# A per-token factor sent to all partitions through DRAM in place of TensorE transposes, in a streaming encoder layer

## The chip, the cores and the metric

The kernel runs on one NeuronCore of one Trainium2 chip. The metric is the device time of one launch, in microseconds (us); the median of 3 runs before the change is 784.9 us (784.69 to 785.13). Engines: PE is TensorE (PEld its weight loads), DVE VectorE, ACT ScalarE, POOL GpSimd, and SP SyncE, which issues all DMAs of this kernel from one queue, in order.

## The reference

One post-norm layer over 2048 prompt frames and 128 sample frames (8 streams of 16), width 1024. One input projection feeds three branches; their gated results are concatenated and go through one output projection. Branch C is the one that the change touches:

```python
h = jnp.einsum('btd,de->bte', x, w_in)
a, g_a, u, v, g_b, c1, c2, g_c = jnp.split(h, SPLITS, axis=-1)
...
c = c1 * jax.nn.sigmoid(c2)
conv_ext = jnp.concatenate([conv_left.astype(c.dtype), c], axis=1)
y_c = conformer_tail(conv_ext, conv_w, conv_b, conv_ln_g, conv_ln_b, conv_pw_w, conv_pw_b)
...
def conformer_tail(ext, conv_w, conv_b, ln_g, ln_b, pw_w, pw_b):
    y = lax.conv_general_dilated(ext, conv_w[:, None, :].astype(ext.dtype), (1,), 'VALID',
                                 dimension_numbers=('NWC', 'WIO', 'NWC'),
                                 feature_group_count=D_CONV) + conv_b
    y = jax.nn.silu(layer_norm(y, ln_g, ln_b))
    return jnp.einsum('btc,ce->bte', y, pw_w) + pw_b
```

The convolution has 31 taps for each of the 384 channels. The layer norm over the channels needs, for each token, the factor 1/sigma = (var + eps)^-0.5 of them.

## The kernel before

**Tiles and blocks.** The 17 tiles of 128 tokens are cut into three blocks (6, 6 and 5 tiles; 768, 768 and 640 tokens). In a block the projection runs over 8 groups of weight columns: groups 0 and 1 make `c1` and `c2` (`ps_c`), 2 and 3 branch A (`ps_ga`, `ps_a`), 4 to 6 branch B, 7 the gate of C. Every product is made of three (high x high, low x high, high x low: L208, L209, L210), since the operands are split into two parts. PE writes the 512-column PSUM banks of the pool `psm`, of which there are six. A last stage runs the output projection tile by tile (`ps_o`, 16 weight slices x 3 products of 512 columns a tile), adds, normalises (L413 to L424, gain and bias on DVE) and stores `o_y`.

**Branch C.** Channels lie on the partitions. DVE does the 31 taps (`acc` from `cext`, and from `cexts` for the sample tokens, so that block 2 has two rows of taps that take turns). What follows the convolution of a block, its tail, is put between the products of the next block, and block 2's tail between those of the output stage. `tail_steps` yields its steps, and `spread` emits one of them every 3.9 us of modelled PE time (4.4 us in the output stage). A tail works on two halves of its block (384 tokens each; 256 in the last half of block 2):

- `sums`, `centre`: sum over the three channel tiles, a product with ones for the mean (`ps_mean`), centred values `dc`, their squares on ACT (`csq`) and the sum of these on DVE (`csqs`).
- `variance` (L572 to L595): for each 128 tokens a product of `csqs` as weights with one column of ones gives the sum over channels in a column of `ps_var`, token by token on the partitions (L577). ACT scales and adds eps (`cvar`, L588), POOL raises to the power -0.5 (L589), and ACT writes each token's number across a row of 128 (`crs`, L594).
- `scale` (L597 to L605): PE transposes `crs`, 128 tokens at a time (`ps_rstd`, L600), so that the numbers lie along the free dimension on all partitions, and DVE multiplies `dc` by them.
- `gate`, `pointwise`: SiLU on ACT, split into `shi` and `slo`, products `ps_pw`, store into `mix`.

The steps were in the order: variance of half 0, an empty step, scale of half 0, variance of half 1, an empty step, scale of half 1. `one` puts its one-column products 0.2 us of modelled time apart, so that long products come between them.

**What sets the order.** Each engine runs its instructions in the order in which the program emits them. `after(us, fn)` emits work when the modelled PE time has come that far. Nothing moves while the kernel runs: an instruction that waits holds up all behind it on its engine, and a DMA that waits holds up all behind it on SP. Weights of later blocks come back from DRAM (`whi<-keep`, `wlo<-keep`, L195) into a ring of 6 buffers, the first half of each odd group into `stage`.

The lines that the steps below name: L131 is the helper that records every DVE operation, L152 the ACT half of a split, L195 the loads of kept weights, L952 the loads of `mix`, L1021 POOL's addition of the bias to `xr`.

Of the kernel before, what the change touches and what calls it, by code (L numbers as in the profile page):

```python
# [9 lines left out]
F32 = mybir.dt.float32  # L10
F32R = mybir.dt.float32r
AF = mybir.ActivationFunctionType
ALU = mybir.AluOpType

D = 1024
P = 128
# [44 lines left out]
def splits(total):  # L61

    tiles = total // P
    n = -(-tiles // 3)
    out, t = [], 0
    for i in range(n):
        w = -(-(tiles - t) // (n - i))
        out.append((t * P, w * P))
        t += w
    return out  # L70
# [3 lines left out]
def encoder_kernel(ctx: ExitStack, tc: tile.TileContext, a):  # L74
    nc = tc.nc
# [5 lines left out]
    pst = ctx.enter_context(tc.tile_pool(name="pst", bufs=2, space=PS))  # L81
    dram = ctx.enter_context(tc.tile_pool(name="dram", bufs=1, space=bass.MemoryType.DRAM))
# [13 lines left out]
    def after(us, fn):  # L96
        Clock.seq += 1
        heapq.heappush(events, (Clock.pe + us, Clock.seq, fn))
# [35 lines left out]
    vec = Vector()  # L134
# [155 lines left out]
    for k in range(2):  # L290
        nc.vector.tensor_copy(whi0[:, k, :], w0[:, k, :])
        nc.vector.tensor_tensor(out=wlo0[:, k, :], in0=w0[:, k, :], in1=whi0[:, k, :].bitcast(F32),
                                op=ALU.subtract)
# [17 lines left out]
    ident = const.tile([P, P], F32, name="ident")  # L311
# [4 lines left out]
    onef = ones.bitcast(F32)  # L316
# [3 lines left out]
    cp = ctx.enter_context(tc.tile_pool(name="convp", bufs=1))  # L320
# [214 lines left out]
    def tail_steps(b):  # L535

        st = {}
# [34 lines left out]
        def variance(i, t0, n):  # L572

            ps = pst.tile([P, 384], F32, tag="tr", name="ps_var")
            nt = n // P
            def one(t):
                nc.tensor.matmul(ps[:, t:t + 1], st["sq", i][:, t * P:(t + 1) * P], onef[:, 0:1],  # L577
                                 start=True, stop=True)
                if t + 1 < nt:
                    after(0.2, lambda: one(t + 1))  # L580
                else:
                    after(0.4, go)
            v = const.tile([P, 3], F32, tag="cvar", bufs=2, name="cvar")[:, :nt]
            rb = cp.tile([P, 384], F32, tag="s", bufs=2, name="crs").rearrange("p (i t) -> p i t", t=P)
            st["rs", i] = rb

            def go():
                nc.scalar.activation(out=v, in_=ps[:, :nt], func=AF.Identity, scale=1.0 / 384, bias=eps)  # L588
                nc.gpsimd.tensor_tensor(out=v, in0=v, in1=mhalf.to_broadcast([P, nt]), op=ALU.pow)  # L589
                after(1.2, wide)  # L590

            def wide():
                for t in range(nt):
                    nc.scalar.activation(out=rb[:, t, :], in_=onef, func=AF.Identity, scale=v[:, t:t + 1])  # L594
            one(0)  # L595

        def scale(i, t0, n):  # L597
            ps = pst.tile([P, 384], F32, tag="tr", name="ps_rstd")
            for t in range(n // P):
                nc.tensor.transpose(ps[:, t * P:(t + 1) * P], st["rs", i][:, t, :], ident)  # L600

            def go():
                for j in range(3):
                    vec.tensor_tensor(out=d[:, j, t0:t0 + n], in0=d[:, j, t0:t0 + n], in1=ps[:, :n], op=ALU.mult)
            after(0.4, go)  # L605

        def gate(t0, n, j):
            s = cp.tile([P, 384], F32, tag="s", bufs=2, name="s")
# [24 lines left out]
        todo = splits(len(BLOCKS[b]) * P)  # L633
        d = cp.tile([P, 3, TMAX], F32, tag="dc", name="dc")
# [5 lines left out]
            fn()  # L640
        for i, (t0, n) in enumerate(todo):
            yield lambda: variance(i, t0, n)
            yield None
            yield lambda: scale(i, t0, n)
        for t0, n in todo:
            for j in range(3):
# [242 lines left out]
    for b in range(len(BLOCKS)):  # L889
        if b > 0:  # L890
            drain()
            conv_state["held"] = []
            spread(tail_steps(b - 1))
# [24 lines left out]
        elif b < LASTB:  # L918
# [4 lines left out]
            def load(*ks, b=b):  # L923
                for k in ks:
                    rows[k] = XRow(b + 1, k)
# [16 lines left out]
    op = ctx.enter_context(tc.tile_pool(name="outp", bufs=1, reuse_waits="tile"))  # L942
# [128 lines left out]
    for q in range(2):  # L1071
        out_finish(q, both[q], True)
    tail = tail_steps(LASTB)
    nxt = Mixed(3)
    for q in range(2, NTILE):
# [86 lines left out]
```

## Time and profile before

| | |
|---|---|
| median of 3 runs | 784.9 us |
| the profiled execution | 785.07 us |
| its span | 783.4 us |
| mean granted TensorE clock | 0.998 |
| DVE's taps (L131, `acc`) | 270 in the largest group, 258.2 us |
| one-column products (`ps_var`) | 34 passes, median 208 ns |
| transposes (`ps_rstd`) | 17, median 272 ns |
| ACT's rows of 128 (`crs`) | 17, median 388 ns |

The span is what the trace covers; the rest of the time lies around it. The views used below: the busy shares by engine; the chain of work that ended last; the waits by engine; the timeline, in which a row gives the start, the time, the engine, the line, the operation, the result and its sources, how many were merged, and in brackets the idle time before and what ended it; the rows of one tile (minimum/median/maximum ns, first and last start); the DMA issues (how many, KB each, median us from issue to landing). Busy times of PE overlap, since its products are pipelined: what one product costs is read from the distance of the starts.

### The profile page before, as it was taken

How to read it: one execution, taken by the hardware profiler on the slowest of the kernel's cores; microseconds unless marked ns; L12 is line 12 of the kernel's file. 1: busy time of each engine (PE TensorE's matmuls, PEld its weight loads, DVE VectorE, ACT ScalarE, POOL GpSimd, SP SyncE). 2: the span in 40 equal slices, each digit the busy share in tenths (PEclk: the TensorE clock that was granted, in tenths of full speed). 3: DMA queues.
4: the chain of work that ended last, by engine and by line, in shares of the span. 5: the costliest groups of instructions: out<-in, count | busy, mean ns of one | idle time of the engine just before them, and what ended most of it. 6: DMA issues, size and time to landing. Idle time of an engine off the chain costs nothing.

```text
span 783.4 us, 11336 instructions
## 1 busy us (share of the span) xinstructions
PE 771.0 (98%) x4340; PEld 732.5 (94%) x4340; DVE 611.6 (78%) x899; ACT 203.2 (26%) x379; POOL 144.2 (18%) x172
## 2 busy tenths in 40 slices
PE   8999999999999999999999999999999999999996
PEld 6999999999999999999999999999988878888885
DVE  5799999996489989896047888899764997676665
ACT  5322324222312130220142122031351243131210
POOL 1010112210001011230002200151006254232341
PEclk9999999999999999999999999999999999999999
DMA  7966856459531465413656147362377334435311
GB/s 248 342 216 190 284 208 236 159 188 338 183 109 44 90 231 193 161 45 138 228 169 208 47 94 219 144 209 97 134 239 267 108 134 162 161 110 182 128 69 73
DMA packets 74774, 132.91 MB, mean 170 GB/s; under 512 B 15584, under 2 KB 41312, under 8 KB 74720
## 3 DMA queue, kind: packets, MB, share of 16 engines
q1 hardware_dynamic: 74720, 132.19, 50.6%
q8 instruction: 34, 0.56, 0.3%
q14 instruction: 20, 0.16, 0.1%
HBM read 90.52 MB, written 41.64 MB: 169 GB/s over the span
## 4 chain that ended last, share of the span: by engine, by line
PE 87%; DVE 6%; DMA 3%; SPq 1%; issue 1%; ACT 1%; POOL 1%; POOLq 0%; DVEq 0%; ACTq 0%
PE ps_o L209 7%; PE ps_o L208 7%; PE ps_o L210 7%; PE ps_c L208 4%; PE ps_c L209 4%; PE ps_c L210 4%; PE ps_gb L208 3%; PE ps_gc L208 3%; PE ps_gb L209 3%; PE ps_gc L209 3%; PE ps_gc L210 3%; PE ps_gb L210 3%; PE ps_v L208 3%; PE ps_v L209 3%; PE ps_v L210 3%; PE ps_u L210 3%
## 5 line engine op out<-in xcount | busy, mean ns | idle before, releaser
L131 DVE SCALAR_TENSOR_TENSOR acc<-cext,cw,acc 128x768 f32<-128x768 f32 (+1 forms) x270 | 258.2, 956 | 4.2
L209 PE MATMUL ps_o<-woxlo,mhi 128*128 128x512 f32 (+1 forms) x208 | 80.9, 389 | 0.0
L208 PE MATMUL ps_o<-woxhi,mhi 128*128 128x512 f32 (+1 forms) x208 | 80.8, 389 | 0.0
L208 PE MATMUL ps_c<-xhi,whi 128*128 128x384 f32 (+1 forms) x240 | 79.8, 333 | 0.7 <-ACT xhi L152 0.7
L210 PE MATMUL ps_o<-woxhi,mlo 128*128 128x512 f32 (+1 forms) x208 | 80.4, 387 | 0.0
L209 PE MATMUL ps_c<-xlo,whi 128*128 128x384 f32 (+1 forms) x240 | 78.9, 329 | 0.7 <-DVE xlo L131 0.5
L210 PE MATMUL ps_c<-xhi,wlo 128*128 128x384 f32 (+1 forms) x240 | 78.4, 327 | 0.0
L131 DVE TENSOR_TENSOR xlo<-stage,xhi 128x768 fp32r<-128x768 f32 (+2 forms) x26 | 21.5, 853 | 36.5 <-ACT xhi L152 36.5
L208 PEld LDWEIGHTS ps_o<-woxhi,mhi 128*128 128x128 f32 x208 | 39.1, 188 | 8.3 <-ACT sgc L533 0.2
L209 PEld LDWEIGHTS ps_c<-xlo,whi 128*128 128x128 f32 x240 | 45.2, 188 | 1.7 <-DVE xlo L131 1.7
L208 PEld LDWEIGHTS ps_c<-xhi,whi 128*128 128x128 f32 x240 | 45.3, 189 | 1.6 <-ACT xhi L152 1.3
L210 PEld LDWEIGHTS ps_o<-woxhi,mlo 128*128 128x128 f32 x208 | 39.1, 188 | 8.1
L208 PE MATMUL ps_u<-whi,xhi 128*128 128x384 f32 x136 | 46.6, 342 | 0.0
L209 PEld LDWEIGHTS ps_o<-woxlo,mhi 128*128 128x128 f32 x208 | 39.1, 188 | 7.6
L424 ACT ACTIVATE xr<-xr,onm,ors 128x1024 f32<-128x1024 f32 x16 | 19.9, 1245 | 101.1 <-POOL onm L420 101.1
L210 PE MATMUL ps_u<-whi,xlo 128*128 128x384 f32 x136 | 45.5, 335 | 0.0
L209 PE MATMUL ps_v<-wlo,xhi 128*128 128x384 f32 x136 | 45.5, 334 | 0.0
L208 PE MATMUL ps_v<-whi,xhi 128*128 128x384 f32 x136 | 45.5, 334 | 0.0
L210 PE MATMUL ps_v<-whi,xlo 128*128 128x384 f32 x136 | 45.5, 334 | 0.0
L209 PE MATMUL ps_u<-wlo,xhi 128*128 128x384 f32 x136 | 45.4, 334 | 0.0
L210 PEld LDWEIGHTS ps_c<-xhi,wlo 128*128 128x128 f32 x240 | 45.2, 188 | 0.0
L131 DVE TENSOR_TENSOR xr<-xr,ln_g 128x1024 f32<-128x1024 f32 x16 | 28.5, 1783 | 20.0 <-ACT xr L424 20.0
(212 smaller groups left out, 1944.2 us busy)
## 6 DMA issues: line engine op xcount, KB each, us to landing
whi<-keep SPq DMA_DIRECT2D x34, 384.0 KB, 5.8
wlo<-keep SPq DMA_DIRECT2D x34, 384.0 KB, 6.4
stage<-in_w_in SPq DMA_DIRECT2D x27, 384.0 KB, 5.0
keep<-whi SPq DMA_DIRECT2D x24, 384.0 KB, 3.9
keep<-wlo SPq DMA_DIRECT2D x24, 384.0 KB, 4.1
xr<-in_x_prompt SPq DMA_DIRECT2D x16, 512.0 KB, 5.0
o_y<-xr SPq DMA_DIRECT2D x16, 512.0 KB, 2.9
stage<-keep SPq DMA_DIRECT2D x20, 384.0 KB, 7.6
```

Source lines behind the costliest of these rows:

```text
L131: return fn(*args, **kw)
L208: nc.tensor.matmul(ps, lh, rh, start=(k == 0), stop=False)
L209: nc.tensor.matmul(ps, lh, rl, start=False, stop=False)
L210: nc.tensor.matmul(ps, ll, rh, start=False, stop=(k == kdim - 1))
L424: nc.scalar.activation(out=out, in_=src, func=AF.Identity, scale=rs, bias=nm_)
```

## The change

The way of 1/sigma from a column of numbers, one token to a partition, to rows on all partitions changes. ACT's rows and PE's transposes go. In their place SP writes the column to DRAM (`crow`, a row of 384 numbers, one number at a time) and reads that row back into all 128 partitions (`crs`). DVE multiplies by `crs` in SBUF where it read `ps_rstd` in PSUM. The one-column products of a half are emitted in one go. The steps are now: variance of half 0, variance of half 1, two empty steps, scale of half 0, scale of half 1; there are six as before, so all later steps keep their places.

```diff
-            def one(t):
+            for t in range(nt):
                 nc.tensor.matmul(ps[:, t:t + 1], st["sq", i][:, t * P:(t + 1) * P], onef[:, 0:1],
                                  start=True, stop=True)
-                if t + 1 < nt:
-                    after(0.2, lambda: one(t + 1))
-                else:
-                    after(0.4, go)
             v = const.tile([P, 3], F32, tag="cvar", bufs=2, name="cvar")[:, :nt]
-            rb = cp.tile([P, 384], F32, tag="s", bufs=2, name="crs").rearrange("p (i t) -> p i t", t=P)
-            st["rs", i] = rb
+            row = dram.tile([3, P], F32, name=f"crow{b}_{i}")
 
             def go():
                 nc.scalar.activation(out=v, in_=ps[:, :nt], func=AF.Identity, scale=1.0 / 384, bias=eps)
                 nc.gpsimd.tensor_tensor(out=v, in0=v, in1=mhalf.to_broadcast([P, nt]), op=ALU.pow)
-                after(1.2, wide)
+                after(1.5, wide)
 
             def wide():
-                for t in range(nt):
-                    nc.scalar.activation(out=rb[:, t, :], in_=onef, func=AF.Identity, scale=v[:, t:t + 1])
-            one(0)
+
+                with nc.allow_non_contiguous_dma(reason="a number for each token"):
+                    nc.sync.dma_start(out=row[:nt].rearrange("t p -> p t"), in_=v)
+
+                def load():
+                    rb = cp.tile([P, 384], F32, tag="s", bufs=2, name="crs")[:, :n]
+                    nc.sync.dma_start(out=rb, in_=row[:nt].rearrange("t p -> (t p)").partition_broadcast(P))
+                    st["rs", i] = rb
+                after(2.5, load)
+            after(0.4, go)
 
         def scale(i, t0, n):
-            ps = pst.tile([P, 384], F32, tag="tr", name="ps_rstd")
-            for t in range(n // P):
-                nc.tensor.transpose(ps[:, t * P:(t + 1) * P], st["rs", i][:, t, :], ident)
-
-            def go():
-                for j in range(3):
-                    vec.tensor_tensor(out=d[:, j, t0:t0 + n], in0=d[:, j, t0:t0 + n], in1=ps[:, :n], op=ALU.mult)
-            after(0.4, go)
+            for j in range(3):
+                vec.tensor_tensor(out=d[:, j, t0:t0 + n], in0=d[:, j, t0:t0 + n], in1=st["rs", i], op=ALU.mult)
...
         for i, (t0, n) in enumerate(todo):
             yield lambda: variance(i, t0, n)
-            yield None
+        yield None
+        yield None
+        for i, (t0, n) in enumerate(todo):
             yield lambda: scale(i, t0, n)
```

The lines behind L606 move up by four or two (L952 is L950 after the change). Three places of the new order follow; a number behind a name tells buffers apart.

PE, block 1, the first half of block 0's tail (`ps_var` are the one-column products). Before:

```order
L210 MATMUL ps_c<-xhi_1977,wlo 128x384
L577 MATMUL ps_var<-ones,csqs 128x1
L208 MATMUL ps_c<-xhi_1977,whi 128x384
L209 MATMUL ps_c<-xlo_1978,whi 128x384
L210 MATMUL ps_c<-xhi_1977,wlo 128x384
L577 MATMUL ps_var<-ones,csqs 128x1
L208 MATMUL ps_c<-xhi_2015,whi 128x384
```

After:

```order
L210 MATMUL ps_c<-xhi_1977,wlo 128x384
L577 MATMUL ps_var<-ones,csqs 128x1 x3
L208 MATMUL ps_c<-xhi_1977,whi 128x384
L209 MATMUL ps_c<-xlo_1978,whi 128x384
L210 MATMUL ps_c<-xhi_1977,wlo 128x384
```

The three one-column products stand together now; those of the second half stand 24 long products behind them (30 in block 2, 21 in the output stage), where before they came behind the first scale's transposes, which are gone.

SP, block 2, where the weights of group 2 (`keep_0_436` to `keep_6_439`) are fetched behind the `stage` loads of group 1. Before:

```order
L195 DMA stage<-keep_0_218 128x768 x2
L195 DMA stage<-keep_2_219 128x768 x2
L195 DMA whi<-keep_0_436 128x2x256
L195 DMA wlo<-keep_0_436 128x2x256
L195 DMA whi<-keep_2_437 128x2x256
```

After:

```order
L195 DMA stage<-keep_2_219 128x768 x2
L590 DMA crow_0_4145<-cvar 128x3x1
L594 DMA crs<-crow_0_4145 128x384
L590 DMA crow_1_4199<-cvar 128x3x1
L195 DMA whi<-keep_0_436 128x2x256
L195 DMA wlo<-keep_0_436 128x2x256
L195 DMA whi<-keep_2_437 128x2x256
L195 DMA wlo<-keep_2_437 128x2x256
L195 DMA whi<-keep_4_438 128x2x256
L195 DMA wlo<-keep_4_438 128x2x256
L594 DMA crs<-crow_1_4199 128x384
L195 DMA whi<-keep_6_439 128x2x256
```

Three of the four new DMAs stand ahead of the first weight pair, the fourth ahead of the last pair (in block 1 ahead of the second). In the output stage they stand between `xr`, `o_y` and the loads of `mix`.

DVE, block 1 (`acc` are the taps, `dc` the values that are scaled). Before:

```order
L131 SCALAR_TENSOR_TENSOR cext_2228<-cext_2228,ps_c 128x384
L131 TENSOR_TENSOR dc<-dc,ps_rstd 128x384 x3
L131 SCALAR_TENSOR_TENSOR acc_2273<-cext_2081,cw,acc_2273 128x768 x2
L131 SCALAR_TENSOR_TENSOR cext_2228<-cext_2228,ps_c 128x384
L131 SCALAR_TENSOR_TENSOR acc_2273<-cext_2081,cw,acc_2273 128x768 x8
L131 TENSOR_TENSOR dc<-dc,ps_rstd 128x384 x3
```

After:

```order
L131 SCALAR_TENSOR_TENSOR cext_2228<-cext_2228,ps_c 128x384
L131 SCALAR_TENSOR_TENSOR acc_2273<-cext_2081,cw,acc_2273 128x768 x3
L131 SCALAR_TENSOR_TENSOR cext_2228<-cext_2228,ps_c 128x384
L131 SCALAR_TENSOR_TENSOR acc_2273<-cext_2081,cw,acc_2273 128x768 x4
L131 TENSOR_TENSOR dc<-dc,crs 128x384 x3
L131 SCALAR_TENSOR_TENSOR acc_2273<-cext_2081,cw,acc_2273 128x768 x2
L131 TENSOR_TENSOR dc<-dc,crs 128x384 x3
L131 SCALAR_TENSOR_TENSOR acc_2273<-cext_2081,cw,acc_2273 128x768 x3
```

The first scale moves seven taps back, the second stays near its place. In block 2 seven pairs of taps stand ahead of the first scale and two behind it, where before the first scale stood ahead of them and nine pairs followed. In the output stage the first scale stands one tile later than before, ahead of the split of the next `mix` tile.

## The prediction

> **What bounds the kernel now.** I read the busy shares first, then the shares of the chain that ended last, then all the waits of PE.
>
> ```profile
> PE 771.0 (98%) x4340; PEld 732.5 (94%) x4340; DVE 611.6 (78%) x899; ACT 203.2 (26%) x379; POOL 144.2 (18%) x172
> PE 87%; DVE 6%; DMA 3%; SPq 1%; issue 1%; ACT 1%; POOL 1%; POOLq 0%; DVEq 0%; ACTq 0%
> PE ps_rstd L600 <- ACT crs L594: 1.2, 1, 1.2
> ```
>
> PE is busy for 98% of the span, is 87% of the chain, and the one wait of PE that this change touches is the 1.2 us for `crs`. So the question is what the change takes out of PE's own stream and what new wait it puts in; DVE, ACT, POOL and SP count only where they make PE wait. The profiled execution took 785.07 us (783.4 us of span and 1.67 us around it), 0.17 us over the median of 784.9 us; I work out differences and take them off the median.
>
> **What leaves PE.** Places in the first tail (block 0's, during block 1) and the last:
>
> ```profile
> 219.32 0.33 PE L209 MATMUL ps_c<-xlo,whi 128*128 128x384 f32 x1
> 220.53 0.34 PE L210 MATMUL ps_c<-xhi,wlo 128*128 128x384 f32 x1
> 220.71 0.28 PE L577 MATMUL ps_var<-ones,csqs 128*128 128x1 f32 x2
> 221.28 0.34 PE L210 MATMUL ps_c<-xhi,wlo 128*128 128x384 f32 x1
> 229.53 0.34 PE L210 MATMUL ps_c<-xhi,stage 128*128 128x384 f32 x1
> 229.71 0.49 PE L600 MATMUL ps_rstd<-ident,crs 128*128 128x128 f32 x3
> 230.39 0.33 PE L210 MATMUL ps_c<-xhi,stage 128*128 128x384 f32 x1
> 633.32 0.39 PE L210 MATMUL ps_o<-woxhi,mlo 128*128 128x512 f32 x1
> 635.38 0.39 PE L210 MATMUL ps_o<-woxhi,mlo 128*128 128x512 f32 x1
> 636.95 0.91 PE L600 MATMUL ps_rstd<-ident,crs 128*128 128x128 f32 x3 [1.19 <-ACT crs L594]
> 638.16 0.40 PE L210 MATMUL ps_o<-woxhi,mlo 128*128 128x512 f32 x1
> 652.38 0.40 PE L210 MATMUL ps_o<-woxhi,mlo 128*128 128x512 f32 x1
> 653.29 0.40 PE L210 MATMUL ps_o<-whi,mlo 128*128 128x512 f32 x1
> ```
>
> The busy times overlap, so I use starts. A 384-column product costs (220.53 - 219.32) / 7 = 0.173 us, a 512-column one (635.38 - 633.32) / 9 = 0.229 us. From one L210 to the next there are three of them, the rest is what was put between:
> - three transposes in flow: 230.39 - 229.53 - 3 x 0.173 = **0.34 us**, 0.113 each. There are four such triples (two in block 1, two in block 2): 1.36 us.
> - the last triple, which waits: 638.16 - 635.38 - 3 x 0.229 = **2.09 us**, wait included.
> - the last pair: 653.29 - 652.38 - 0.69 = **0.22 us**.
>
> All 17 are gone in the order of the change: 1.36 + 2.09 + 0.22 = **3.67 us** off PE.
>
> **The one-column products.** One of them costs 221.28 - 220.53 - 0.52 = 0.23 us, in two passes of 0.115 us. A transpose beside two others costs 0.113 us, a pass beside one other 0.115 us: a short pass costs the same whatever stands next to it. So 17 products x 0.23 us stay as dear when they follow one another, and I take **0**. Six short passes in a row don't occur in this trace, so both ends stay open.
>
> ```profile
> L577 PEld LDWEIGHTS ps_var<-ones,csqs x34: 187/188/192, 220.5 to 643.5; 128*128 128x128 f32 x34
> ```
>
> Dear end: each weight load shows its full 0.188 us, 6 x (0.188 - 0.115) = 0.44 us a triple, 2.5 us for 34 passes. Cheap end: the start times of the 0.23 us split into 0.13 us of passes and 0.10 us at the return to long products; then a triple saves two returns, and five triples and a pair save about 1.1 us.
>
> **What is late next: the second product of the last tail.** The second variance step moves ahead of the first scale. In the last tail its 2 products come 21 long products behind the first three, instead of after the scale.
>
> ```profile
> 625.29 0.28 PE L577 MATMUL ps_var<-ones,csqs 128*128 128x1 f32 x2
> 630.61 0.43 DVE L131 TENSOR_TENSOR csqs<-csqs,csq 128x256 f32<-128x256 f32 x1
> ```
>
> PE gets there at 625.29 + 3 x 0.23 + 21 x 0.229 = 630.79, and its weights are the squares that DVE finishes at 631.04. The weight load, else hidden behind the product before, starts then; I estimate **0.45 us** of new wait (0.25 for the data, the rest for the load and its signal), from 0 to 0.9. DVE and PE both run on from the same product there, so the difference of their times should hold. In blocks 1 and 2 DVE has both halves' squares done before the first product, so nothing waits there.
>
> Sum: -3.67 + 0.45 = **-3.2 us**, if nothing of the new way through DRAM reaches PE.
>
> **The new way, step by step.** `crow` writes 384 numbers one by one; `crs` reads 1.5 KB to each of 128 partitions.
>
> ```profile
> o_conv_p<-ncs SPq DMA_DIRECT2D x3, 15.0 KB, 1.7
> o_pool_s<-aexts SPq DMA_DIRECT2D x2, 60.0 KB, 7.3
> stage<-in_conv_pw_w SPq DMA_DIRECT2D x3, 192.0 KB, 2.8
> vg<-in_gmlp_ln_g SPq DMA_DIRECT2D x1, 192.0 KB, 7.9
> whi<-keep SPq DMA_DIRECT2D x12, 256.0 KB, 4.0
> wlo<-keep SPq DMA_DIRECT2D x12, 256.0 KB, 4.7
> ```
>
> `o_conv_p` is 128 pieces, `o_pool_s` 1024 pieces (of 60 B): 384 pieces lie between, in proportion 1.7 + 5.6 x 256 / 896 = **3.3 us** for `crow`, with ends of 1.7 and 7.3. `crs` has the form of `vg` (one row to all partitions, 192 KB): **7.9 us**, low end 2.8. The Trainium skill (DMA: Bandwidth & Descriptors, "Anatomy of one DMA") gives about 2.0 us fixed plus bytes at 436 GB/s, fitted on another issue path; an estimate by it is 2.0 and 2.5 us, and the sum would be the same -3.2 us, with more room.
>
> Behind `crow` and `crs` on SP stand the loads of group 2's weights, the DMAs most at risk, since SP waits for POOL's power, then for `crow` to land.
>
> ```profile
> 222.86 1.19 POOL L589 TENSOR_TENSOR cvar<-cvar,mhalf 128x3 f32<-128x3 f32 x1 [5.88 <-ACT cvar L588]
> 243.74 1.48 DVE L131 TENSOR_TENSOR dc<-dc,ps_rstd 128x384 f32<-128x384 f32 x3 [0.92 <-PE ps_rstd L600]
> 245.14 2.07 DVE L131 SCALAR_TENSOR_TENSOR acc<-cext,cw,acc 128x768 f32<-128x768 f32 x2
> 251.36 0.33 PE L208 MATMUL ps_ga<-xhi,whi 128*128 128x384 f32 x1
> ```
>
> Block 1: the first power ends at 224.05, `crow` lands at 227.4, `crs` at 235.4; by the order of the change DVE reaches the second scale one tap sooner than before (243.74 - 0.92 - 1.0 = 241.8) and the first one three multiplies and two taps ahead of that, at 238.2. The second power ends near 227.5 (its products follow the first ones by 24 long ones, 4.2 us), its `crow` goes out near 228 and lands at 231.3, its `crs` at 239.3, wanted at 241.8. The first weight pair goes out behind that `crow`, the other three behind that `crs`, by 235 (SP takes some 0.5 us for each DMA); they land by 240, and PE wants them at 251.36. All hidden.
>
> ```profile
> 423.47 4.66 POOL L589 TENSOR_TENSOR cvar<-cvar,mhalf 128x3 f32<-128x3 f32 x1 [6.29 <-ACT cvar L588]
> 428.55 0.56 DVE L131 SCALAR_TENSOR_TENSOR cext<-cext,ps_c 128x384 f32<-128x384 f32 x1 [1.13 <-PE ps_c L210]
> 431.82 1.48 DVE L131 TENSOR_TENSOR dc<-dc,ps_rstd 128x384 f32<-128x384 f32 x3
> 437.44 4.89 POOL L589 TENSOR_TENSOR cvar<-cvar,mhalf 128x3 f32<-128x3 f32 x1 [5.25 <-ACT cvar L588]
> 443.60 0.56 DVE L131 SCALAR_TENSOR_TENSOR cext<-cext,ps_c 128x384 f32<-128x384 f32 x1 [1.98 <-ACT cext L474]
> L208 PE MATMUL ps_ga<-xhi,whi x24: 277/308/339, 446.5 to 470.4; 128*128 128x384 f32 x12, 128*128 128x256 f32 x12
> ```
>
> Block 2: the power takes 4.7 and 4.9 us, four times block 1's. Both times it ends 0.71 us after DVE falls idle (428.55 - 1.13 = 427.42 to 428.13, 443.60 - 1.98 = 441.62 to 442.33): DVE's two interleaved rows of taps keep it out. The new second power starts at 428.13, with 0.42 us of idle DVE left, then a DVE step that reads PSUM (0.56 us); I take it to end there, near 429. Then: `crow` out at 428.2, landed at 431.5, `crs` at 439.4 (DVE did nine pairs of taps from 433.3 to 441.62, 0.92 us each; now seven from 431.82, so it wants `crs` at 438.3 and waits 1 us); the second `crow` 432 to 435.4; three pairs of weight loads out by 435, landed by 440; the second `crs` 435.4 to 443.3, wanted 1.48 + 2 x 0.92 + 0.8 us behind the first, near 443.5; the last weight pair out by 436.5, landed by 441.2. PE starts on them at 446.5 less 0.7, 445.8. Hidden, and 1 us of DVE is covered by six PSUM banks that take PE 24 x 0.173 = 4.2 us each.
>
> ```profile
> 634.62 1.84 POOL L589 TENSOR_TENSOR cvar<-cvar,mhalf 128x3 f32<-128x3 f32 x1
> 637.42 1.25 SPq L952 DMA_DIRECT2D stage<-mix  x2
> 649.37 1.25 DVE L131 TENSOR_TENSOR mlo<-stage,mhi 128x768 fp32r<-128x768 f32 x2
> ```
>
> Last tail: `crow` goes out when POOL's power ends at 636.46, `crs` near 640, landing by 648; DVE wants it at 649.37, where the order puts the first scale, ahead of this split. The loads of `mix` go out 3 us later than 637.42 and are split at 649.37 plus the scale's 1.5 us, with some 6 us to the tile of PE that they are for (a tile is 48 x 0.229 = 11 us). Hidden. ACT loses 17 steps of 0.39 us off the path: worth 0.
>
> **Rivals.**
> - *SP holds up the weights of block 2 (slower).* If the second power gets no gap at 428, DVE leaves none until it waits for the second `crs` itself, near 442.4: the power ends near 443.1, the first weight pair lands at 448.8 (PE waits 3.0 us), `crow` lands between 446.5 and 450.5 (3.3 and 7.3 us), the last pair 5.9 us behind it, wanted at 451.9 by then: 0.5 to 4.5 us more. Together 3.5 to 7.5, middle 5.5 us: **787.2 us**. It decides once the second `crow` lands later than 443.0 (448.9, when PE wants the last pair, less 5.9); above I have 435.4. For it: the two rows of 4.7 and 4.9 us. Against it: the gap at 428.13 and block 1's 1.19 us under the same DVE load. The Trainium skill (SBUF — State Buffer, on the shared port pair) says that a DVE step with two SBUF inputs locks a GpSimd step out for one whole instruction, whoever starts first; by that a power would wait 0.75 us at most and this rival could not happen, and the sum stays -3.2 us. The 4.7 us of the trace speak against so short a wait, so I keep a chance of **0.08**.
> - *The new wait is larger (no change).* If DVE slips before 631.04, PE waits for the squares by as much. The same add took 2.71 us beside a POOL step and 0.56 us without:
>
> ```profile
> 604.87 2.71 DVE L131 TENSOR_TENSOR csum<-acc,acc 128x384 f32<-128x384 f32 x1
> 607.62 0.56 DVE L131 TENSOR_TENSOR csum<-csum,acc 128x384 f32<-128x384 f32 x1
> ```
>
>   One more such meeting costs 2.15 us: **783.9 us**. The dear end of the one-column products (784.2 us) goes with it. Against it: DVE's order ahead of that place is unchanged. Chance **0.15**.
> - *Followed products are cheaper*: the cheap end above, **780.6 us**. Against it: the pair of transposes costs 0.22 us, not less than two thirds of the triple. Chance **0.07**.
>
> **How the numbers follow.** The forecast, 784.9 - 3.2 = **781.7 us**, has **0.70**. About 0.2% (1.6 us) is what a measurement of this kernel can tell from no change. The forecast and the cheap case are faster, 0.77; the larger wait is mostly within 0.2%: 0.14; slower 0.09. The range runs from 780.6 to 784.6 us: it takes in the cheap end, the dear end and the larger wait, and leaves out the held-up weights and half of what is beyond either end.
>
> **What would show it.** Right: no `ps_rstd`; PE's triples of one-column products cost near 0.69 us from L210 to L210 beyond the long ones; one PE wait under 1 us on `csqs` near 630; `ps_ga` of block 2 starts without a wait; `crs` lands ahead of its multiplies, or DVE waits 1 us. Wrong: a PE wait on `whi` or `wlo` near 446, a power of over 5 us in block 2, `crow` over 7 us, or a product triple over 1 us.

## The result and the profile after

The changed kernel takes **795.09 us** (median of 4 runs, 791.37 to 795.83) against 784.99 us before in the same session: ratio 1.012, 95% interval 1.0103 to 1.0137. It is slower by some 10 us, where 781.7 us was forecast and 784.6 us was the top of the range. The profiled execution took 795.83 us, the median within 0.1%.

The first view of the changed kernel is its page: busy shares of the engines, and the chain that ended last.

```profile
PE 773.2 (97%) x4323; PEld 732.2 (92%) x4323; DVE 609.9 (77%) x899; ACT 197.9 (25%) x362; POOL 142.8 (18%) x172
PE 79%; DMA 9%; DVE 6%; issue 3%; POOL 2%; ACT 1%; SPq 0%; POOLq 0%; DVEq 0%; ACTq 0%
```

The 17 transposes are gone (4340 products before, 4323 now), yet PE is busy 2.2 us longer, and DMA has gone from 3% to 9% of the chain. So products ran slower somewhere, and transfers are now waited for. The waits, of all engines and of SP's queue, say for which (an engine and its line, the releaser, then us in total, times, longest):

```profile
PE ps_ga L208 <- DMA whi<-keep: 3.5, 2, 2.6
PE ps_pw L209 <- DVE slo L131: 2.9, 2, 1.5
PE ps_o L208 <- ACT mhi L152: 1.7, 1, 1.7
...
DVE dc L131 <- DMA crs<-crow: 18.3, 4, 7.4
...
SPq L594 <- DMA crow<-cvar: 48.7, 6, 9.6
```

None of these five waits was among the rows of before. The last is the largest: SP, which issues the DMAs of this kernel in order, stands 48.7 us in all before the six `crs`, each time until `crow` has landed. The list of DMA issues of the changed kernel (KB each, median us from issue to landing) has the duration on which the prediction rested:

```profile
crow<-cvar SPq DMA_DIRECT2D x5, 1.5 KB, 9.3
crow<-cvar SPq DMA_DIRECT2D x1, 1.0 KB, 9.6
crs<-crow SPq DMA_DIRECT2D x5, 192.0 KB, 5.2
```

`crow`, 1.5 KB, takes nearly twice as long as `crs`, 192 KB. The timeline of SP's queue (start us, duration, instruction) in block 2 and in the last tail:

```profile
428.67 0.37 SPq L590 DMA_DIRECT2D crow<-cvar  x1
436.78 0.32 SPq L594 DMA_DIRECT2D crs<-crow  x1
437.19 0.39 SPq L590 DMA_DIRECT2D crow<-cvar  x1
437.63 0.48 SPq L195 DMA_DIRECT2D whi<-keep  x1
...
440.45 0.80 SPq L195 DMA_DIRECT2D wlo<-keep  x1
448.92 0.33 SPq L594 DMA_DIRECT2D crs<-crow  x1
449.31 0.43 SPq L195 DMA_DIRECT2D whi<-keep  x1
...
642.94 0.38 SPq L590 DMA_DIRECT2D crow<-cvar  x1
643.48 0.37 SPq L1047 DMA_DIRECT2D o_y<-xr  x1
653.24 0.32 SPq L594 DMA_DIRECT2D crs<-crow  x1
653.61 0.90 SPq L950 DMA_DIRECT2D stage<-mix  x2
```

The second `crow` of block 2 leaves at 437.19 and the `crs` behind it at 448.92, so `crow` landed 11.6 us after its issue. Three weight pairs go out right behind that `crow`, from 437.63 on; the last pair waits with SP until 449.31. In the last tail the loads of `mix` wait from 643.85 to 653.61. What the late weights cost is more than the wait: the sums by stretch (us, then busy time of each engine, granted clock, DMA share, GB/s) show PE at half its clock for 3 us behind it.

```profile
446.50:449.14 2.64, 0.04 (x1) 0.03 (x1) 0.19 (x1) 0.00 (x0) 0.00 (x0) 0.96 0.95 169
449.14:452.20 3.06, 3.06 (x10) 3.06 (x11) 0.00 (x0) 0.00 (x0) 0.00 (x0) 0.50 1.02 161
```

The first weight load was issued at 437.63, and PE starts on it at 449.14: 11.5 us, for a transfer that took 4.0 us (median) before. DMA's busy share in that stretch is 0.95, but it moves only 169 GB/s. Keep this second oddity in mind beside SP's wait.

With products matched between the two traces (same tile, same order, the one-column products and transposes left out), the lead or lag of PE shows where the time went:

| place | start before | start after | lag |
|---|---|---|---|
| end of block 1's tail | 243.45 | 242.42 | -1.03 |
| `ps_pw`, block 1 (scale late) | 261.43 | 261.83 | +0.41 |
| last `ps_c` of block 2 | 445.35 | 445.30 | -0.05 |
| `ps_ga`, first weights | 446.51 | 449.14 | +2.63 |
| `ps_ga`, last weights | 449.99 | 455.64 | +5.65 |
| `ps_o`, waits for ACT's `sgc` | 577.91 | 584.87 | +6.96 |
| last tail, where the transposes stood | 637.62 | 643.12 | +5.50 |
| `ps_o`, waits for `mix` (`mhi`, `mlo`) | 658.11 | 665.19 | +7.08 |
| `ps_pw`, last tail (scale late) | 672.77 | 681.61 | +8.84 |
| end | | | +10.63 |

The largest step, 5.7 us, is at block 2's weights; the late `mix` gives some 2 us, the late scales 1.4 us in block 1 and 1.8 us in the last tail. No wait stands behind the last rise, from +8.84 to the end: there (737 to 780) a 512-column product takes 0.233 us in the place of 0.229, at a granted clock of 1.00. The profiled executions of e1 and e9 below show the same 0.233 us there, the other kernels' 0.229 us, so it comes and goes with the execution; why, no run shows.

### The profile page after: what moved, and what is told of

It is laid out like the page before. It is cut to its first block, busy times and chain, and to the rows that moved or that the text cites. A ratio compares the mean times of both kernels' runs of the same rounds, so it can differ in the third digit from the quotient of the medians.

```text
span 794.1 us, 11303 instructions
## 1 busy us (share of the span) xinstructions
PE 773.2 (97%) x4323; PEld 732.2 (92%) x4323; DVE 609.9 (77%) x899; ACT 197.9 (25%) x362; POOL 142.8 (18%) x172
## 4 chain that ended last, share of the span: by engine, by line
PE 79%; DMA 9%; DVE 6%; issue 3%; POOL 2%; ACT 1%; SPq 0%; POOLq 0%; DVEq 0%; ACTq 0%
PE ps_o L210 5%; PE ps_o L208 5%; PE ps_o L209 5%; PE ps_c L209 4%; PE ps_c L208 4%; PE ps_c L210 4%; DMA crow<-cvar 4%; PE ps_gb L208 3%; PE ps_gb L209 3%; PE ps_gb L210 3%; PE ps_v L208 3%; PE ps_v L210 3%; PE ps_v L209 3%; PE ps_u L208 3%; PE ps_u L210 3%; PE ps_u L209 3%
## 5 line engine op out<-in xcount | busy, mean ns | idle before, releaser
L208 PEld LDWEIGHTS ps_o<-woxhi,mhi 128*128 128x128 f32 x208 | 39.2, 188 | 11.6 <-ACT mhi L152 2.1
L479 POOL COPY halo_c<-cext 128x30 f32<-128x30 f32 x9 | 4.5, 500 | 223.5 <-DVE cext L131 223.5
```

What stands on the lines that cost most here:

```text
L208: nc.tensor.matmul(ps, lh, rh, start=(k == 0), stop=False)
L479: nc.gpsimd.tensor_copy(halo_c[:, j, :], ext[:, Tp:Tp + CONVC])
```

## The experiments

**Theory 1**: `crow`'s landing of 8.0 to 11.6 us holds SP, and the weights, the loads of `mix` and the scales behind it are late. **Theory 2**: the new order of the steps, or the products that follow one another, cost the time. **Theory 3**: it isn't the form of `crow`; any small write costs as much. The first four kernels ran together, beside the kernel before at 784.94 us.

**e1, rows of three.** The changed kernel, with `crow` laid out as `cvar` lies.

```diff
-            row = dram.tile([3, P], F32, name=f"crow{b}_{i}")
+            row = dram.tile([P, nt], F32, name=f"crow{b}_{i}")
...
-                    nc.sync.dma_start(out=row[:nt].rearrange("t p -> p t"), in_=v)
+                    nc.sync.dma_start(out=row, in_=v)
...
-                    nc.sync.dma_start(out=rb, in_=row[:nt].rearrange("t p -> (t p)").partition_broadcast(P))
+                    nc.sync.dma_start(out=rb, in_=row.rearrange("p t -> (p t)").partition_broadcast(P))
...
-                vec.tensor_tensor(out=d[:, j, t0:t0 + n], in0=d[:, j, t0:t0 + n], in1=st["rs", i], op=ALU.mult)
+                x = d[:, j, t0:t0 + n].rearrange("q (t p) -> q t p", p=P)
+                vec.tensor_tensor(out=x, in0=x, in1=st["rs", i].rearrange("q (p t) -> q t p", p=P), op=ALU.mult)
```

> The changed kernel, but crow is laid out as it lies in cvar: one piece of 12 bytes for each partition, side by side, so 128 pieces in the place of 384 of 4 bytes; crs reads the same 192 KB, and the scale's multiplies read crs with a stride of three. Theory 1 (the landing of crow, 8.0 to 11.6 us, holds SP's queue, and the weights of block 2, the loads of mix and the late scales wait behind it): crow lands in 2 to 5 us, the 2.8 us wait of ps_ga for whi at 446 goes, and the time falls to 781 to 785 us. Theory 2 (the order of the steps or the products that follow one another cost the time): it stays at 794 to 796 us. Theory 3 (any write of this kernel into DRAM out of the const pool takes some 9 us, whatever its pieces): crow still lands in 8 to 10 us and the time stays above 792 us. If the strided read makes the multiplies slower, they take more than the 0.5 us each that they had.

Measured: 782.14 us, ratio 0.9971 (0.9958 to 0.9983). The chain on its page (shares of the span by engine):

```profile
PE 95%; DMA 3%; ACT 1%; DVE 0%; issue 0%; SPq 0%; POOLq 0%; DVEq 0%; POOL 0%; ACTq 0%
```

and its list of DMA issues:

```profile
crow<-cvar SPq DMA_DIRECT2D x5, 1.5 KB, 2.2
crow<-cvar SPq DMA_DIRECT2D x1, 1.0 KB, 8.0
```

The same numbers, the same DMAs in the same order on the same queue; only where the 384 numbers lie has changed, and some 12 us are gone (the ratio went from 1.012 to 0.9971, with the intervals above). PE's wait for `whi` is gone too, and PE is 95% of the chain (87% before, 79% in the changed kernel). Theory 3 falls: the same bytes land in 2.2 us at the median, in four of the six writes in 2.0 to 2.2 us. This kernel beats both others, though by little: the interval against the kernel before leaves 1.3 to 3.3 us. The strided multiplies take 0.67 us each (median) in the place of 0.55, hidden on DVE. The other two writes of `crow` took 6.9 us, right behind a `crs` in block 2, and 8.0 us, right behind the loads of `mix`: in this form too a write can land late under traffic, but PE did not wait for what stood behind these two.

**e2, the order alone.** The kernel before, transposes kept, with only the order of the change.

```diff
-            def one(t):
+            for t in range(nt):
                 nc.tensor.matmul(ps[:, t:t + 1], st["sq", i][:, t * P:(t + 1) * P], onef[:, 0:1],
                                  start=True, stop=True)
-                if t + 1 < nt:
-                    after(0.2, lambda: one(t + 1))
...
-            yield None
+        yield None
+        yield None
+        for i, (t0, n) in enumerate(todo):
             yield lambda: scale(i, t0, n)
```

> The kernel before with the order part of the change alone: the one-column products follow one another, the second variance stands ahead of the first scale; 1/sigma still goes through the transposes and no number goes to DRAM. Theory 1 (the way through DRAM costs the time): 783 to 786 us, about that of the kernel before; the 1.2 us wait for crs in the last tail shrinks, and a new wait for csqs of some 0.4 us comes in. Theory 2 (order or consecutive products cost the time): 790 us or more.

Measured: 783.85 us, ratio 0.9982 (0.9973 to 0.9992). Theory 2 falls. The order alone is worth 0.6 to 2.1 us: the last tail's wait for `crs` (1.19 us before) has gone without any DRAM, because the scale comes later there. No wait for `csqs` of 0.3 us or more appears.

**e4, the read later.** The changed kernel, `crs` issued later, so that block 2's weights go ahead of both.

```diff
-                after(2.5, load)
+                after(8, load)
```

> The changed kernel with crs issued 5.5 us of TensorE work later (8 in the place of 2.5 after crow), so that in block 2 both crow and the weight loads stand ahead of both crs on SP; the landing of crow is not changed. Theory 1, in the form that SP waits at crs for crow and holds what is behind it: the wait of ps_ga for whi at 446 goes, which is worth some 5 us there; the scales come later and may cost some of it back at ps_pw. Expected 788 to 793 us. If the weights were late for another reason (the engines of the DMA rings being busy with 4-byte pieces, say), the wait stays and the time is 794 us or more.

Measured: 798.06 us, ratio 1.0173 (1.0145 to 1.0201), a miss: not faster at all. Waits of PE:

```profile
PE ps_o L210 <- DVE mlo L131: 5.2, 1, 5.2
PE ps_pw L209 <- DVE slo L131: 5.1, 2, 2.7
```

The wait for `whi` has gone as theory 1 has it (the product that lagged at 454.92 starts 4.2 us sooner than in the changed kernel). In its place the second `crs` of the last tail now holds SP until 660.82, with the next loads of `mix` behind it, and PE waits 5.2 us there. Whatever stands behind the waiting read pays. One thing was not expected: the weight loads, now issued behind both `crow` with no read between that waits, landed 12.4 us (median of `whi`) after their issue.

**e3, forms of the write in place.** The kernel before, with one unread write of `cvar` in each tail half, six forms.

```diff
+                    if (b, i) == (0, 0):
+                        w = dram.tile([3, P], F32, name="w0")
+                        nc.sync.dma_start(out=w.rearrange("t p -> p t"), in_=v)
+                    elif (b, i) == (0, 1):
+                        w = dram.tile([P, 3], F32, name="w1")
+                        nc.sync.dma_start(out=w, in_=v)
...
```

> The kernel before with one more write into DRAM per tail half, which nobody reads: the same numbers of cvar in six forms, each once: 384 pieces of 4 bytes packed (the form of crow), 128 pieces of 12 bytes side by side, 384 of 4 bytes 64 bytes apart, 256 of 4 bytes 512 bytes apart, 128 of 4 bytes packed, 128 of 8 bytes 64 bytes apart (the last two halves' forms as the tail's size allows). If the number of pieces sets the landing (my first estimate, in proportion, with 384 pieces now at 9.3): 9, 3, 9, 9, 3, 3 us. If pieces that share a line of DRAM hinder one another: the packed ones 9 and 3 or more for the fourth, those 64 or 512 bytes apart 3 us or less. If any piece under some size is slow, whatever the number: all six 8 us or more. The time of this kernel itself is not read.

Measured, in the order of the forms: 11.4, 6.8, 2.4, 1.6, 9.9 and 4.5 us, one sample each and with other traffic around it. 128 packed pieces are nearly as slow as 384, and 384 pieces that lie apart are fast: number and size of the pieces don't decide. This needed a quiet place, which the next run gives.

**e5, the forms alone.** Behind the last instruction of the kernel before, on idle DMAs, 11 forms, three times each, each followed by a read that waits for it.

```diff
+        for rep in range(3):
+            w = dram.tile([3, P], F32, name=f"packed384_{rep}")
+            nc.sync.dma_start(out=w.rearrange("t p -> p t"), in_=v[:, 0:3])
+            nc.sync.dma_start(out=v[0:1, 0:1], in_=w[0:1, 0:1])
+            w = dram.tile([3, P, 2], F32, name=f"pitch8_{rep}")
+            nc.sync.dma_start(out=w[:, :, 0].rearrange("t p -> p t"), in_=v[:, 0:3])
+            nc.sync.dma_start(out=v[0:1, 0:1], in_=w[0, 0:1, 0:1])
...
```

> The kernel before, and behind its last instruction, on idle DMAs, a chain of writes of 1/sigma-like numbers into DRAM in 11 forms, three times each; each write is followed by a read of 4 bytes that waits for it, so that no two overlap. The rival readings of what makes crow slow: (a) the number of pieces: all forms of 384 pieces take the same 8 us or more, those of 128 pieces a third of it; (b) pieces of under 64 bytes, however they lie: all but the rows of 64 bytes are slow; (c) pieces that share a short line of DRAM follow one another: 384 packed pieces and 128 packed pieces take the same 8 to 10 us, the landing falls in proportion as the pieces are moved apart (pitch 8, 16, 32 bytes) and is 2 us from 64 bytes on, with the 12-byte rows side by side at 3 us or less; (d) the traffic around crow, not its form: all take about 2 us here. From the six single writes of the run before I expect (c). The time of this kernel itself is not read.

The trace by line; each line's issues (min/median/max ns, first and last start) and its landings, for 384 packed pieces, pieces 8 bytes apart, pieces 64 bytes apart, 128 packed pieces, and 128 rows of 12 bytes:

```profile
L1094 SPq DMA_DIRECT2D packed<-v x3: 379/380/412, 781.3 to 885.7; - x3
DMA to landing us min/median/max: 8.3/8.5/10.4
...
L1097 SPq DMA_DIRECT2D pitch<-v x3: 380/380/401, 792.8 to 896.8; - x3
DMA to landing us min/median/max: 2.7/4.2/4.3
...
L1106 SPq DMA_DIRECT2D pitch<-v x3: 373/374/378, 805.4 to 908.4; - x3
DMA to landing us min/median/max: 1.7/1.7/1.8
...
L1115 SPq DMA_DIRECT2D packed<-v x3: 341/341/342, 814.0 to 917.1; - x3
DMA to landing us min/median/max: 7.5/7.6/8.9
...
L1118 SPq DMA_DIRECT2D rows<-v x3: 341/342/342, 824.6 to 927.7; - x3
DMA to landing us min/median/max: 2.1/2.3/2.5
```

All eleven, medians of three:

| pieces | bytes from one to the next | pieces to 64 bytes | landing us |
|---|---|---|---|
| 384 of 4 bytes | 4 | 16 | 8.5 |
| 384 of 4 bytes | 8 | 8 | 4.2 |
| 384 of 4 bytes | 16 | 4 | 2.9 |
| 384 of 4 bytes | 32 | 2 | 2.0 |
| 384 of 4 bytes | 64, 128, 512 | 1 | 1.7 |
| 128 of 4 bytes | 4 | 16 | 7.6 |
| 128 of 12 bytes | 12 | 5.3 | 2.3 |
| 128 of 12 bytes | 64 | 1 | 1.4 |
| 128 of 64 bytes | 64 | 1 | 1.4 |

The landing follows the number of pieces that share 64 bytes, some 0.45 us for each beyond the first ((8.5 - 1.7) / 15), as if they had to follow one another; 64 bytes apart, 384 pieces land in 1.7 us. The rows of 12 bytes are cheaper than this proportion (3.4 us by it, from 1.4 us); why, no run shows. Reading (c) stands. The Trainium skill (DMA: Bandwidth & Descriptors, "Specifications") says that transfers under 512 bytes are done by read-modify-write. The trace agrees that small pieces can hinder one another, but not with 512 bytes as the unit: a pitch of 64 bytes, eight pieces to 512 bytes, lands as soon as a pitch of 512 (1.7 us both).

**e6 and e7, the slow write put back, and its twin.** To e1 an unread write is added with a read of 4 bytes of it ahead of `crs`; in e6 in 384 packed pieces, in e7 in as many pieces 64 bytes apart (`w` is a tile of `[3, P, 16]` there, written at `w[:nt, :, 0]`). The kernel before took 785.29 us beside them.

```diff
+                    w = dram.tile([3, P], F32, name=f"w{b}_{i}")
+                    nc.sync.dma_start(out=w[:nt].rearrange("t p -> p t"), in_=v)
...
+                    z = const.tile([1, 1], F32, tag="z", bufs=2, name="z")
+                    nc.sync.dma_start(out=z, in_=w[0:1, 0:1])
```

> The faster layout (crow in 128 rows of 12 bytes), and beside it on SP what crow did: an unread write of the same numbers in 384 packed pieces of 4 bytes, and ahead of crs a read of 4 bytes of it, which waits for it. Theory 1 (SP, waiting for a slow write, is what costs the time, and the slowness comes from pieces that share lines): 791 to 797 us, with the wait of ps_gap for whi near 446 back. Should the time stay under 785 us, SP's waiting is not the cause.

> As the run with the packed dummy, but the 384 pieces of 4 bytes of the dummy lie 64 bytes apart; as many pieces, DMAs and waits of SP, nothing shares a line of 64 bytes. Theory 1 with the shared lines: the dummy lands in 2 to 4 us and the time is 782 to 785 us. If the number of pieces or of DMAs on SP is what costs: 791 us or more, like the run beside it.

Measured: e6 792.62 us, ratio 1.0095 (1.008 to 1.011); e7 781.29 us, ratio 0.995 (0.9933 to 0.9967). The waits of PE in e6:

```profile
PE ps_ga L208 <- DMA whi<-keep: 3.6, 1, 3.6
```

The unread write in the list of DMA issues of e6:

```profile
w<-cvar SPq DMA_DIRECT2D x5, 1.5 KB, 9.7
```

and in that of e7:

```profile
w<-cvar SPq DMA_DIRECT2D x5, 1.5 KB, 4.1
```

The two kernels differ in nothing but the distance between the pieces of a write whose content nobody uses: 11.3 us. (e7 came out 0.7 us below the range named for it, and its write at 4.1 us just above.)

**e8, another queue.** The changed kernel with `crow` and `crs` on POOL's queue, so that SP is free.

```diff
-                    nc.sync.dma_start(out=row[:nt].rearrange("t p -> p t"), in_=v)
+                    nc.gpsimd.dma_start(out=row[:nt].rearrange("t p -> p t"), in_=v)
...
-                    nc.sync.dma_start(out=rb, in_=row[:nt].rearrange("t p -> (t p)").partition_broadcast(P))
+                    nc.gpsimd.dma_start(out=rb, in_=row[:nt].rearrange("t p -> (t p)").partition_broadcast(P))
```

> The changed kernel with crow and crs issued from POOL's queue in the place of SP's; the form of crow stays. Theory 1 (what costs the time is what stands behind crow on SP): the waits of ps_ga for whi at 446 and the late loads of mix in the last tail go, the scales stay late: 785 to 790 us, if POOL's own work behind the waiting crs (the other half's power, add_bias and onm) isn't wanted sooner. If the late scales alone cost the time: 793 us or more.

Measured: 803.52 us, ratio 1.0206 (1.0147 to 1.0265), a miss. The profiled execution was the fastest of the four, 794.22 us; the others took 802.5 to 805.0. The waits of PE, to start with:

```profile
PE ps_o L210 <- DVE mlo L131: 4.8, 1, 4.8
```

The timeline of POOL in the last tail (in brackets the idle time before, and what ended it):

```profile
652.78 0.60 POOL L594 DMA_DIRECT2D crs<-crow  x1 [10.34 <-issue]
653.38 0.73 POOL L590 DMA_DIRECT2D crow<-cvar  x1
654.18 0.19 POOL L413 TENSOR_SCALAR ors<-omv 128x1 f32<-128x1 f32 x1
```

The timeline of DVE there:

```profile
656.71 2.14 DVE L131 TENSOR_TENSOR xr<-xr,ln_g 128x1024 f32<-128x1024 f32 x1 [11.97 <-ACT xr L424]
```

The wait of PE for `whi` isn't among them, so that half of theory 1 holds. But `crow` is no faster there (8.1 to 11.3 us), and POOL stands 10.34 us before `crs`, with the output's own 1/sigma (`ors`) behind it; DVE then waits 11.97 us for ACT's `xr`, and its split of `mix` comes 4.8 us too late for PE. The wait is not SP's; it belongs to whichever queue holds the read. This accounts for the 794 us of the profiled execution; what the other three lost beyond it, no trace shows.

**e9 and e10, the two halves of the cost.** Two rows were left unexplained: the 11.5 us of the weights behind `crow`, and the 12.4 us in e4, where no read held SP ahead of them. So there may be two effects: SP's wait (1a), and a stop in the DMA engines for what is queued behind the slow write (1b). e9 is e6 without its read, so that no read waits for the slow write:

```diff
+                    w = dram.tile([3, P], F32, name=f"w{b}_{i}")
+                    nc.sync.dma_start(out=w[:nt].rearrange("t p -> p t"), in_=v)
```

e10 is e1 with a wait of SP but no slow write, a chain of five single pieces ahead of `crs`:

```diff
+                    z = const.tile([1, 3], F32, tag="z", bufs=2, name="z")
+                    w = dram.tile([2, 1], F32, name=f"w{b}_{i}")
+                    nc.sync.dma_start(out=z[:, 0:1], in_=row[0:1, 0:1])
+                    for r in range(2):
+                        nc.sync.dma_start(out=w[r:r + 1], in_=z[:, r:r + 1])
+                        nc.sync.dma_start(out=z[:, r + 1:r + 2], in_=w[r:r + 1])
```

> The faster layout of crow in rows of 12 bytes, and beside it the unread write of 384 packed pieces of 4 bytes, but nothing reads it, so SP never waits for it. The run with the packed dummy and a read that waits took 792.6 us; this one has the write alone. In the trace of the changed kernel the weight loads of block 2 that were issued 0.4 us behind crow landed 11.6 us later, with packets of 1 KB that took up to 2.7 us, so the slow write may also stop what stands behind it in the DMA engines. Theory 1a (only SP's waiting costs): weights land 6 to 8 us after their issue as without the dummy, 781 to 785 us. Theory 1b (the slow write also stops the DMAs behind it): the weight loads of block 2 land 10 to 12 us after their issue, crs, which stands behind it too, lands in some 8 us or more in the place of 5.8, and the time is 784 to 792 us.

> The faster layout, and ahead of crs on SP a chain of five DMAs of 4 bytes each (read, write, read, write, read), each waiting for the one before: SP stands some 8 us more at each crs, as in the changed kernel, but no write has pieces that share a line. Theory 1a (SP's waiting alone): the wait of ps_ga for whi near 446 and the late loads of mix come back, 789 to 796 us. Theory 1b (what the slow write stops in the DMA engines is the larger part): the weights are issued as late as in the changed kernel, but land in 6 us, in time, and the time is 782 to 788 us, from the late scales and mix alone.

Measured: e9 789.53 us, ratio 1.0055 (1.0035 to 1.0075); e10 790.42 us, ratio 1.0061 (1.004 to 1.0083). Each alone costs most of e6's loss. The waits of PE in e9:

```profile
PE ps_ga L208 <- DMA whi<-keep: 4.8, 1, 4.8
```

`crs` in its list of DMA issues:

```profile
crs<-crow SPq DMA_DIRECT2D x5, 192.0 KB, 9.9
```

A wait of SP's queue in e9:

```profile
SPq L195 <- DMA w<-cvar: 15.7, 3, 7.0
```

The waits of PE in e10:

```profile
PE ps_ga L208 <- DMA whi<-keep: 5.7, 1, 5.7
```

The timeline of SP there, in block 2:

```profile
435.83 0.42 SPq L195 DMA_DIRECT2D whi<-keep  x1
...
440.37 0.24 SPq L595 DMA_DIRECT2D z<-crow  x1
...
449.34 0.42 SPq L195 DMA_DIRECT2D whi<-keep  x1
```

In e9 the first three weight pairs of block 2 were issued from 435.31 on, and those whose landing the trace has took 16.1 to 16.7 us, where e1's took 6.4 to 7.5; `crs` takes 9.9 us in the place of 5.8. PE waited for the first of these loads, which landed at 451.36. With e1's 6.4 us it would have been there at 441.7, so 1b is real. But SP is not free in e9: three times, 15.7 us in all, it stands before a weight load until `w` has landed, though the load doesn't touch it. The `whi` of 448.59, the eighth DMA behind the `w` of 434.52, is one of them. In e4 the loads of 439.43 and 440.95, the eighth behind each `crow`, likewise start just when that `crow` has landed (439.37 and 440.88). So a slow write, even one that nobody reads, holds SP at the eighth DMA behind it. These waits came behind the pair for which PE waited; their own share of e9's time is not separated. In e10 the first three pairs were in time; the last pair, issued at 449.34 behind SP's second wait, was not: 1a is real too. The four cells:

| | no slow write | slow write |
|---|---|---|
| no added read for which SP waits | e1, 782.1 us | e9, 789.5 us |
| an added read for which SP waits | e10, 790.4 us | e6, 792.6 us |

They don't add up; both make weights of the same group late (e9 the first pair, e10 the last, e6 the first).

## Why the prediction was wrong

**The step that failed** is the landing of `crow`: "384 pieces lie between, in proportion 1.7 + 5.6 x 256 / 896 = 3.3 us for `crow`, with ends of 1.7 and 7.3". Measured: 8.0 to 11.6 us in the kernel, 8.5 us on idle DMAs, beyond the dear end. The number of pieces was the wrong measure: the two neighbouring rows had pieces of 60 bytes or more, of which at most two share 64 bytes, and `crow` has sixteen. With 3.3 us the timetable gave 435.4 for the second `crow`'s landing in block 2; it was 448.8. "Hidden" rested on that, for block 2's weights and the last tail's `mix`.

**The rival that came true in part.** "SP holds up the weights of block 2" was to decide "once the second `crow` lands later than 443.0". It landed at 448.8, and PE did wait at 446.5 for the first weights and once more for the last pair. But I let it start from POOL's power, and this was in time: 428.13 to "near 429" was forecast, and in the changed kernel both powers are done by 429.46 (the row merges them: 5.4 and 0.85 us).

```profile
423.26 6.20 POOL L584 TENSOR_TENSOR cvar<-cvar,mhalf 128x3 f32<-128x3 f32 x2 [5.58 <-ACT cvar L583]
```

Its price, 5.5 us, was close to the 5.7 us of that place, but in part by luck: it has waits of 3.0 and 2.5 us, and the trace shows waits of 2.6 and 0.9 us and most of the rest from the halved clock. It had no term for the slow weights behind the write, for the clock halved after the wait, for the `mix` loads, or for the scales of both tails; hence 795 and not 787.2 us.

**What held.**
- *Transposes out.* With the slow write away, the forecast of -3.2 us (a ratio of 0.9959) lies within the intervals of e1 and e7, toward opposite ends of them. Of the 3.67 us, the wait of 1.19 us needed only the order (e2).
- *Products that follow one another: 0.* In the timeline of PE in the changed kernel three of them, in six passes, take 221.29 - 220.10 - 3 x 0.173 = 0.67 us; forecast 0.69.

```profile
220.10 0.34 PE L210 MATMUL ps_c<-xhi,wlo 128*128 128x384 f32 x1
220.27 0.72 PE L577 MATMUL ps_var<-ones,csqs 128*128 128x1 f32 x6
...
221.29 0.34 PE L210 MATMUL ps_c<-xhi,wlo 128*128 128x384 f32 x1
```

- *The new wait for `csqs`, 0.45 us*: too dear. In the changed kernel the pair takes no more than its two products (638.77 - 637.62 - 3 x 0.229 = 0.46 us); in e1 and e6 the wait is 0.2 us, in e2 below 0.3. Within its bounds.
- *`crs`, 7.9 us with a low end of 2.8*: 5.2 us, 3.5 to 6.0. Too dear, within its bounds, and without effect.
- *The signs named beforehand* ("a PE wait on `whi` or `wlo` near 446", "`crow` over 7 us") were the ones that appeared. A third, "a power of over 5 us in block 2", appeared too (5.4 us) but cost nothing: e1 and e7, which are faster than the kernel before, have the same 5.4 us.

One step of the table above stays open: the 1.2 us at 577.91, where PE waits for ACT's `sgc`. It appears in e1 too, less in e7 (0.3 us of wait), and not in e2. In the changed kernel's ACT timeline, casts of `mix` and `w_out` come in another order against `sgc` there; I didn't try to separate it.

## What to carry to other kernels

Before a small write into DRAM is called hidden, ask how many of its pieces share 64 bytes, and compare only with rows of the trace that do the same; write the numbers as they lie in SBUF, side by side or 64 bytes apart, and let the reader take the stride. A read that waits for a write holds everything queued behind it, whichever queue it is on, so list what that is and when it is wanted. A slow write also delays the transfers that are queued behind it in the DMA engines, even where nothing reads it, and on SP's queue the eighth DMA behind it waited for it (e4, e9).

## What the hardware did that I had not expected

- **4-byte writes packed side by side land 8.3 to 10.4 us after their issue on idle DMAs, and 1.7 us when 64 bytes apart** (e5), although the packets themselves start within 0.5 us and show 7 to 9 ns each.
- **Such a write delays others.** From 437.6 to 452.4 in the changed kernel, 57 of 1536 packets of 1 KB, 46 ns at the median, took over 0.5 us, up to 2.7 us. In e1, while the same weights were fetched (432.3 to 444.4), 12 of 2048 did, one of them 3.1 us, so a single long packet says little. DMA moved 147 GB/s from 446 to 448, against 379 GB/s from 438 to 440 in e1. In which part of the way the packets are held, no run shows.
- **The clock halves after a short wait, for 3.4 or 6.8 us at a time.** 2.6 us without products were followed by 3.1 us at a clock of 0.50, which added about 1.5 us. In e6 a wait of 3.6 us goes with a granted clock of 0.50 from 447.7 to 454.5 (products at half their rate from 448.49 to 454.38), and a wait of 2.2 us at `ps_pw` with 0.51 from 679.8 to 683.2; in e8 1.9 us were enough. In e4 waits of 2.4 and 2.7 us at `ps_pw` were not followed by any. So the length of the wait alone doesn't decide. The Trainium skill (TensorE: Matmul & The Clock Gate, "What's actually happening") has the clock fall after an idle window of some 3.4 us that runs freely; the half rate agrees, but here 1.9 to 2.6 us were enough three times, and 2.4 and 2.7 us were not at two others.
